# A decoder block in split precision: a padded low part of k, and the two softmax components combined on ScalarE and GpSimd

## The chip, the cores and the metric

The kernel runs on one core of one Trainium2 chip. The time is that of one execution on the device in microseconds (us): the median of several runs, and for a profile the span from the first to the last instruction.

A core has five engines that matter here. TensorE (PE) multiplies matrices; its weight loads are listed apart (PEld). VectorE (DVE), ScalarE (ACT) and GpSimd (POOL) work on tiles of up to 128 partitions. SyncE (SP) and ACT issue the DMAs. Each engine works through its instructions in order.

## The reference, cut to what matters

The input is 512 rows of 1024 numbers, in float32. After a norm, one projection gives a convolution branch, q and k (8 heads with two components of 64 each), v (8 heads of 128) and two gates. The part around the change is the differential attention:

```python
def diff_attention(q, k, v, lam):
    for i in range(seq_len // Q_BLOCK):          # 4 blocks of 128 queries
        kv_len = (i + 1) * Q_BLOCK
        s = jnp.einsum("bqhcd,bkhcd->bhcqk", qs, ks).astype(jnp.float32) * scale
        s = jnp.where(mask, s, neg)
        p = jax.nn.softmax(s, axis=-1)
        a = p[:, :, 0] - lam * p[:, :, 1]        # two components, 64 numbers each
        outs.append(jnp.einsum("bhqk,bkhe->bqhe", a.astype(v.dtype), vs))
```

Then the heads are normed and projected, gated together with the convolution branch (31 taps per channel, a layer norm, SiLU, a projection), projected, and a feed-forward layer of 2816 and a last norm follow.

## The kernel before

*Split precision.* A float32 matrix is kept as a high part (rounded to the matmul's format, fp32r) and a low part (the rest), and a product is three matmuls: high by high, low by high, high by low. Weights arrive in units of 512 KB (tile wr); ACT casts the high part (wh), and POOL (for units 3 to 63) or DVE subtracts for the low part (wl), three units ahead of their use (`next_unit`, lines 341 to 348).

*Stages.* The convolution's input projections; then eight heads, each with its q and k projection and, every second head, a v projection; the gates, with the norm of the heads; the projections; the feed-forward layer. The convolution's taps (one DVE instruction each, from `conv_ops`) fill DVE through the heads.

*The scores.* For a head, `softmaxes` (lines 610 to 675) packs high and low of q into one tile of 128 rows per component: qs2[c] has the high part of q in its own 64 rows and the low part in the other 64. kd[c] holds the high part of k twice. So one matmul of 128 rows gives high by high plus low by high. The third product, high of q by low of k, is a matmul of 64 rows (line 641), since kl holds both components, 64 rows each. A block i has (i+1) x 128 columns and four such matmuls, two for each component.

*The softmax.* For each component DVE adds the mask and takes the row maximum in one instruction (line 644, a custom one in the profile), multiplies the maximum by -0.125 (a one-column TENSOR_SCALAR), and ACT takes the exponential and its sum. `combine` then has two reciprocals, one multiplication by lambda (lamc), a multiplication of component 1 on ACT, and the combination on DVE (line 664). `outputs` transposes the result on PE, splits it (ACT and DVE) and multiplies by v.

*What sets the order.* Python generators with a model of each engine's clock (class `Model`, lines 80 to 121, costs in `Engine`, lines 142 to 162) record the program: a generator yields until the model says that its operands are ready, and `pump` puts taps on DVE whenever its modelled clock falls behind PE's. So fewer or cheaper instructions on one engine move others as well. Nothing is reordered on the chip.

Of the kernel before, what the change touches and what calls it, by code (L numbers as in the profile page):

```python
# [4 lines left out]
T = 512  # L5
D = 1024
P = 128
NH = 8
HD = 64
# [158 lines left out]
def build(nw):  # L168
# [10 lines left out]
    nc = bacc.Bacc("TRN2", target_bir_lowering=False, num_devices=1)  # L179
# [12 lines left out]
    need = model.need  # L192
    clk = model.clk

    with tile.TileContext(nc) as tc, contextlib.ExitStack() as homes:
# [3 lines left out]
        with tc.tile_pool(name="cn", bufs=1) as cn, \  # L199
# [88 lines left out]
            def until_room(tag, n, reserve=0):  # L288
                while live[tag] + n + reserve > BUFS[tag]:
                    yield now[0] + 0.3  # L290
# [164 lines left out]
            G.memset(mhalf, -0.5)  # L455
            make_identity(nc, ident)
# [153 lines left out]
            def softmaxes(h, qk):  # L610
                yield need(*qk)

                qm, km = qk
                yield from until_room("T4", 5)
                qs2 = [tl("T4", F32R) for _ in range(2)]
                kd = [tl("T4", F32R) for _ in range(2)]
                kl = tl("T4", F32R)
# [4 lines left out]
                for c in range(2):  # L622
                    S.copy(kd[c][half[1 - c]], km[half[c]])
                    V.tensor_tensor(out=qs2[c][half[1 - c]], in0=qm[half[c]], in1=f32(qs2[c])[half[c]], op=ALU.subtract)
                    V.tensor_tensor(out=kl[half[c]], in0=km[half[c]], in1=f32(kd[c])[half[c]], op=ALU.subtract)
# [5 lines left out]
                def scores(i):  # L631
                    kv = (i + 1) * P
                    pm, rs = [], []
                    for c in range(2):
                        cp = slice(c * HD, (c + 1) * HD)
                        qs = slice(i * P, (i + 1) * P)
                        yield from until_room("T5", 1, 5)
                        s_ps = psum("at")
                        yield need(s_ps, qs2[c], kd[c], kl)
                        mm(s_ps[:, :kv], qs2[c][:, qs], kd[c][:, :kv], True, False)  # L640
                        mm(s_ps[:, :kv], qs2[c][cp, qs], kl[cp, :kv], False, True)
                        sm = tl("T5")
                        mx, den = small(), small()
                        V.tensor_tensor_reduce(out=sm[:, :kv], in0=s_ps[:, :kv], in1=mask[:, T - kv:], op0=ALU.add,
                                               op1=ALU.max, scale=1.0, scalar=-3.4e38, accum_out=mx)
                        V.tensor_scalar(out=mx, in0=mx, scalar1=-0.125, scalar2=None, op0=ALU.mult)
                        S.activation(sm[:, :kv], sm[:, :kv], AF.Exp, bias=mx, scale=0.125, accum_out=den)
                        pm.append(sm)
                        rs.append(den)
                    prob[i] = (pm, rs)  # L650

                def combine(i):
                    kv = (i + 1) * P
                    pm, rs = prob.pop(i)
                    yield need(*rs)
                    for c in (1, 0):
                        r = small()
                        V.reciprocal(r, rs[c])
                        rs[c] = r
                        if c == 1:  # L660
                            V.tensor_tensor(out=r, in0=r, in1=lamc, op=ALU.mult)
                            S.mul(pm[1][:, :kv], pm[1][:, :kv], mul=r)
                    yield need(pm[1])
                    V.scalar_tensor_tensor(out=pm[0][:, :kv], in0=pm[0][:, :kv], scalar=rs[0], in1=pm[1][:, :kv],
                                           op0=ALU.mult, op1=ALU.subtract)
                    drop("T5")
                    probs[h][i] = pm[0]
# [5 lines left out]
                drop("T4", 5)  # L673
# [386 lines left out]
```

## Time and profile before

| | |
|---|---|
| median of 3 runs | 927.87 us (927.46 to 928.8) |
| the profiled execution | 927.44 us |
| its span | 925.1 us |
| busy PE, DVE, ACT, POOL | 903.1, 593.5, 375.9, 261.9 us |
| mean granted TensorE clock | 0.994 |

Busy times overlap, since the engines work beside each other; only the engine that is never idle sets the time by its own work. Nearly all instructions are recorded at line 141 or by one helper, so rows are told apart by tile names: "mm", "at" and "cv" are PSUM tiles (projections, attention, convolution), "T" is any SBUF tile, "sm" a column. A matmul is shown with its start and a modelled length that overlaps the next one; what it costs in a stream is the distance from start to start.

### The profile page before, as it was taken

What the parts mean: (1) busy time and instruction counts of PE and PEld (TensorE: products, weight loads), DVE (VectorE), ACT (ScalarE), POOL (GpSimd) and SP (SyncE); (2) the same over time, 40 slices, a digit from 0 to 9 for tenths busy, and PEclk for the clock granted to TensorE, in tenths of its full rate; (3) what the DMA queues carried; (4) which work ended last, traced back from release to release, by engine and by line L of the source; (5) the groups of instructions that cost most, each with busy time, mean ns of one, the idle gap of its engine ahead of it and who ended that gap; (6) DMA issues with size and microseconds to landing.
All of it is one profiled execution on the core that took longest, in us unless ns stands there. A gap on an engine that the chain in (4) does not pass through costs nothing.

```text
span 925.1 us, 11231 instructions
## 1 busy us (share of the span) xinstructions
PE 903.1 (98%) x4246; PEld 735.4 (79%) x4246; DVE 593.5 (64%) x1048; ACT 375.9 (41%) x615; POOL 261.9 (28%) x211
## 2 busy tenths in 40 slices
PE   8989999999999999999999999999999999999996
PEld 5868888777787777768788888888888888888885
DVE  6599999898899889996766563333443434422422
ACT  7232336565555786444532442323322232311312
POOL 1654465563645526536200001011111111100000
PEclk9899999999999999999999999999999999999999
DMA  7223222121122222222223342222223332322302
GB/s 273 88 81 106 90 92 69 46 91 46 46 70 69 69 69 69 72 89 81 102 79 126 137 137 92 91 91 91 91 91 111 102 107 92 114 91 91 113 24 91
DMA packets 26150, 85.19 MB, mean 92 GB/s; under 512 B 3041, under 2 KB 3809, under 8 KB 26097
## 3 DMA queue, kind: packets, MB, share of 16 engines
q1 hardware_dynamic: 24944, 82.52, 26.6%
q10 hardware_dynamic: 1152, 1.97, 0.6%
q8 instruction: 33, 0.54, 0.2%
q14 instruction: 21, 0.16, 0.1%
HBM read 82.38 MB, written 2.10 MB: 91 GB/s over the span
## 4 chain that ended last, share of the span: by engine, by line
PE 84%; DVE 9%; ACT 2%; issue 2%; POOL 1%; DMA 1%; SPq 0%; POOLq 0%; ACTq 0%; DVEq 0%
PE mm L141 51%; PE at L141 29%; DVE T L141 7%; PE cv L141 4%; ACT T L141 2%; DVE cv L141 1%; POOL wl L141 1%; DVE sm L141 1%; DMA wr<-wall 1%; ACT wh L141 0%; DMA T<-xT 0%; DVE dg L141 0%; SPq L233 0%; POOL T L141 0%; POOL rc L141 0%
## 5 line engine op out<-in xcount | busy, mean ns | idle before, releaser
L141 PE MATMUL mm<-T,wh 128*128 128x512 f32 x1360 | 427.6, 395 | 3.7 <-DVE T L141 3.2
L141 PEld LDWEIGHTS mm<-T,wh 128*128 128x128 f32 x1360 | 250.0, 188 | 60.3 <-issue 4.6
L141 PE MATMUL mm<-T,wl 128*128 128x512 f32 x680 | 265.7, 391 | 0.5 <-DVE wl L141 0.5
L141 POOL TENSOR_TENSOR wl<-wr,wh 128x512 fp32r<-128x512 f32 x122 | 165.2, 1381 | 172.0 <-ACT wh L141 171.1
L141 ACT CAST wh<-wr 128x1024 fp32r<-128x1024 f32 (+1 forms) x148 | 148.7, 1031 | 71.3 <-PE cv L141 35.3
L141 DVE SCALAR_TENSOR_TENSOR cv<-T,vec_sb,cv 128x512 f32<-128x512 f32 x232 | 160.3, 746 | 0.1
L141 POOL TENSOR_TENSOR T<-T,T 128x512 f32<-128x512 f32 x64 | 84.7, 1325 | 253.7 <-DVE T L141 230.9
L141 PE MATMUL at<-T,wh 128*128 128x512 f32 x496 | 154.4, 393 | 0.0
L141 PEld LDWEIGHTS mm<-T,wl 128*128 128x128 f32 x680 | 127.8, 188 | 28.7 <-DVE wl L141 1.0
L141 DVE TENSOR_TENSOR wl<-wr,wh 128x1024 fp32r<-128x1024 f32 (+1 forms) x88 | 102.0, 1186 | 70.1 <-ACT wh L141 69.7
L141 DVE TENSOR_TENSOR T<-T,T 128x512 fp32r<-128x512 f32 (+2 forms) x127 | 101.6, 801 | 58.9 <-ACT T L141 56.8
L141 ACT CAST T<-T 128x512 fp32r<-128x512 f32 (+2 forms) x112 | 67.5, 617 | 132.9 <-POOL T L141 82.1
L141 PEld LDWEIGHTS at<-T,wh 128*128 128x128 f32 x496 | 93.7, 190 | 19.5
L141 DVE TENSOR_TENSOR T<-mm,T 128x512 f32<-128x512 f32 (+1 forms) x76 | 51.7, 682 | 83.3 <-PE mm L141 73.7
L141 PE MATMUL mm<-wh,T 128*128 128x256 f32 (+1 forms) x432 | 101.2, 318 | 0.0
L141 PE MATMUL at<-T,wl 128*128 128x512 f32 x248 | 97.1, 392 | 0.0
L141 ACT ACTIVATE T<-T 128x512 f32<-128x512 f32 (+1 forms) x66 | 40.4, 622 | 131.9 <-DVE T L141 131.9
L141 ACT ACTIVATE T<-T,sm 128x128 f32<-128x128 f32 (+3 forms) x100 | 56.7, 567 | 81.3 <-DVE sm L141 77.5
L141 PEld LDWEIGHTS mm<-wh,T 128*128 128x128 f32 x432 | 73.0, 190 | 7.0 <-issue 1.3
L141 DVE TENSOR_TENSOR T<-at,T 128x512 f32<-128x512 f32 (+4 forms) x59 | 38.0, 649 | 62.4 <-PE at L141 56.1
L141 PE MATMUL at<-T,T 128*128 128x256 f32 (+8 forms) x288 | 68.2, 334 | 1.2 <-DVE T L141 1.2
L141 PE MATMUL mm<-wl,T 128*128 128x256 f32 (+1 forms) x216 | 68.1, 315 | 0.0
(85 smaller groups left out, 641.3 us busy)
## 6 DMA issues: line engine op xcount, KB each, us to landing
wr<-wall SPq DMA_DIRECT2D x145, 512.0 KB, 3.2
T<-xT SPq DMA_DIRECT2D x16, 256.0 KB, 4.6
out<-T ACTq DMA_DIRECT2D x4, 256.0 KB, 2.8
out<-T SPq DMA_DIRECT2D x4, 256.0 KB, 2.6
wr<-wall SPq DMA_DIRECT2D x4, 128.0 KB, 4.4
T<-cs ACTq DMA_DIRECT2D x2, 256.0 KB, 4.7
T<-gfin SPq DMA_DIRECT2D x2, 256.0 KB, 3.6
T<-mask ACTq DMA_DIRECT2D x1, 256.0 KB, 5.1
```

The lines of the kernel that those rows point to most:

```text
L141: r = f(*args, **kw)
```

## The change

The low part of k gets a tile of 128 rows for each component (kz, two sets, used by heads in turn), whose other 64 rows are set to zero once at the start. The matmul of line 641 so has 128 rows in place of 64: the other half of qs2[c] meets zeros. The row maximum is taken as a minimum of the scores times -0.125, so that the separate multiplication goes; both sums of a block share one tile of two columns, with one reciprocal; the multiplication by lambda is a TENSOR_SCALAR; ACT multiplies both components, and POOL subtracts them. The planner asks for four tiles of "T4" in place of five, and waits for the head before the last. The scratch for dynamic DMAs is set to 1024.

```diff
--- before.py
+++ after.py
@@ -176,7 +176,7 @@
     AF, ALU = mybir.ActivationFunctionType, mybir.AluOpType
     AX = mybir.AxisListType
 
-    nc = bacc.Bacc("TRN2", target_bir_lowering=False, num_devices=1)
+    nc = bacc.Bacc("TRN2", target_bir_lowering=False, num_devices=1, dynamic_dma_scratch_size=1024)
     xT_d = nc.dram_tensor("xT", [8, P, T], F32, kind="ExternalInput").ap()
     w_d = nc.dram_tensor("wall", [nw, P, 1024], F32, kind="ExternalInput").ap()
     vec_d = nc.dram_tensor("vec", [P, NVEC], F32, kind="ExternalInput").ap()
@@ -453,6 +453,10 @@
                 G.memset(f32(pick)[:, 9 * h:9 * h + 1], 1.0)
             G.memset(ones, 1.0)
             G.memset(mhalf, -0.5)
+            kz = [[cn.tile([P, T], F32R, name=f"kz{b}{c}") for c in range(2)] for b in range(2)]
+            for b in range(2):
+                for c in range(2):
+                    G.memset(f32(kz[b][c])[(1 - c) * HD:(2 - c) * HD], 0.0)
             make_identity(nc, ident)
             load(vec, vec_d)
             ss = SumSq("T3", V)
@@ -610,11 +614,14 @@
             def softmaxes(h, qk):
                 yield need(*qk)
 
+
                 qm, km = qk
-                yield from until_room("T4", 5)
+                yield from until_room("T4", 4)
+                while started[0] < h - 2:
+                    yield now[0] + 0.5
                 qs2 = [tl("T4", F32R) for _ in range(2)]
                 kd = [tl("T4", F32R) for _ in range(2)]
-                kl = tl("T4", F32R)
+                kl = kz[h % 2]
                 half = [slice(0, HD), slice(HD, P)]
                 for c in range(2):
                     S.copy(qs2[c][half[c]], qm[half[c]])
@@ -622,7 +629,7 @@
                 for c in range(2):
                     S.copy(kd[c][half[1 - c]], km[half[c]])
                     V.tensor_tensor(out=qs2[c][half[1 - c]], in0=qm[half[c]], in1=f32(qs2[c])[half[c]], op=ALU.subtract)
-                    V.tensor_tensor(out=kl[half[c]], in0=km[half[c]], in1=f32(kd[c])[half[c]], op=ALU.subtract)
+                    V.tensor_tensor(out=kl[c][half[c]], in0=km[half[c]], in1=f32(kd[c])[half[c]], op=ALU.subtract)
                 drop("T5", 2)
                 while started[0] < h - 1:
                     yield now[0] + 0.5
@@ -630,39 +637,34 @@
 
                 def scores(i):
                     kv = (i + 1) * P
-                    pm, rs = [], []
+                    pm, den = [], small(2)
                     for c in range(2):
-                        cp = slice(c * HD, (c + 1) * HD)
                         qs = slice(i * P, (i + 1) * P)
                         yield from until_room("T5", 1, 5)
                         s_ps = psum("at")
-                        yield need(s_ps, qs2[c], kd[c], kl)
+                        yield need(s_ps, qs2[c], kd[c], kl[c])
                         mm(s_ps[:, :kv], qs2[c][:, qs], kd[c][:, :kv], True, False)
-                        mm(s_ps[:, :kv], qs2[c][cp, qs], kl[cp, :kv], False, True)
+                        mm(s_ps[:, :kv], qs2[c][:, qs], kl[c][:, :kv], False, True)
                         sm = tl("T5")
-                        mx, den = small(), small()
+
+                        mx = small()
                         V.tensor_tensor_reduce(out=sm[:, :kv], in0=s_ps[:, :kv], in1=mask[:, T - kv:], op0=ALU.add,
-                                               op1=ALU.max, scale=1.0, scalar=-3.4e38, accum_out=mx)
-                        V.tensor_scalar(out=mx, in0=mx, scalar1=-0.125, scalar2=None, op0=ALU.mult)
-                        S.activation(sm[:, :kv], sm[:, :kv], AF.Exp, bias=mx, scale=0.125, accum_out=den)
+                                               op1=ALU.min, scale=-0.125, scalar=3.4e38, accum_out=mx)
+                        S.activation(sm[:, :kv], sm[:, :kv], AF.Exp, bias=mx, scale=-1.0, accum_out=den[:, c:c + 1])
                         pm.append(sm)
-                        rs.append(den)
-                    prob[i] = (pm, rs)
+                    prob[i] = (pm, den)
 
                 def combine(i):
                     kv = (i + 1) * P
-                    pm, rs = prob.pop(i)
-                    yield need(*rs)
+                    pm, den = prob.pop(i)
+                    yield need(den)
+                    r = small(2)
+                    V.reciprocal(r, den)
+                    V.tensor_scalar(out=r[:, 1:2], in0=r[:, 1:2], scalar1=lamc, scalar2=None, op0=ALU.mult)
                     for c in (1, 0):
-                        r = small()
-                        V.reciprocal(r, rs[c])
-                        rs[c] = r
-                        if c == 1:
-                            V.tensor_tensor(out=r, in0=r, in1=lamc, op=ALU.mult)
-                            S.mul(pm[1][:, :kv], pm[1][:, :kv], mul=r)
-                    yield need(pm[1])
-                    V.scalar_tensor_tensor(out=pm[0][:, :kv], in0=pm[0][:, :kv], scalar=rs[0], in1=pm[1][:, :kv],
-                                           op0=ALU.mult, op1=ALU.subtract)
+                        S.mul(pm[c][:, :kv], pm[c][:, :kv], mul=r[:, c:c + 1])
+                    yield need(*pm)
+                    G.tensor_tensor(out=pm[0][:, :kv], in0=pm[0][:, :kv], in1=pm[1][:, :kv], op=ALU.subtract)
                     drop("T5")
                     probs[h][i] = pm[0]
 
@@ -670,7 +672,7 @@
                     yield from scores(i)
                     if i:
                         yield from combine(i - 1)
-                drop("T4", 5)
+                drop("T4", 4)
                 yield from combine(3)
                 started[0] = h
```

On PE the order of the last block of head 0, before (at_ tiles are the scores; T_194 and T_195 are kd, T_196 is kl; mm_1320 is the v projection that runs around it):

```order
L141 MATMUL mm_1320<-wh_1172,T_88_455 128x256
L141 MATMUL at_1397<-T_194_1201,T_192_1199 128x512
L141 MATMUL at_1397<-T_196_1203,T_192_1199 128x512
L141 MATMUL at_1406<-T_195_1202,T_193_1200 128x512
L141 MATMUL at_1406<-T_196_1203,T_193_1200 128x512
L141 MATMUL mm_1320<-wh_1172,T_89_464 128x256
```

And in the changed kernel, where kz_154 and kz_155 stand for kl:

```order
L141 MATMUL mm_1321<-wh_1180,T_83_442 128x256
L141 MATMUL at_1376<-T_194_1209,T_192_1207 128x512
L141 MATMUL at_1376<-kz_154,T_192_1207 128x512
L141 MATMUL at_1383<-T_195_1210,T_193_1208 128x512
L141 MATMUL at_1383<-kz_155,T_193_1208 128x512
L141 MATMUL mm_1321<-wh_1180,T_87_461 128x256
```

The four matmuls stay in place; the second and fourth read another tile.

On DVE the stretch between the score reductions (ISA) of the third and the fourth block of head 0, before (cv_ are convolution taps; T_211 is the combination of the second block):

```order
L141 TENSOR_SCALAR sm_1343<-sm_1343 128x1
L141 RECIPROCAL sm_1348<-sm_1284 128x1
L141 TENSOR_TENSOR sm_1348<-sm_1348,lamc 128x1
L141 RECIPROCAL sm_1352<-sm_1269 128x1
L141 SCALAR_TENSOR_TENSOR cv_888<-T_113_595,vec_sb,cv_888 128x512
L141 TENSOR_TENSOR T_241_1376<-T_202_1243,T_241_1376 64x512
L141 SCALAR_TENSOR_TENSOR cv_840<-T_96_494,vec_sb,cv_840 128x512
L141 SCALAR_TENSOR_TENSOR cv_888<-T_113_595,vec_sb,cv_888 128x512
L141 TENSOR_TENSOR T_245_1380<-T_221_1302,T_243_1378 64x512
L141 TENSOR_TENSOR T_242_1377<-T_202_1243,T_242_1377 64x512
L141 TENSOR_TENSOR T_245_1380<-T_221_1302,T_244_1379 64x512
L141 SCALAR_TENSOR_TENSOR T_211_1267<-T_211_1267,sm_1352,T_215_1282 128x256
```

The same place now, up to the fourth block's reductions:

```order
L141 ISA sm_1340 128x1
L141 RECIPROCAL sm_1343<-sm_1268 128x2
L141 TENSOR_SCALAR sm_1343<-sm_1343,lamc 128x1
L141 SCALAR_TENSOR_TENSOR cv_848<-T_96_502,vec_sb,cv_848 128x512
L141 SCALAR_TENSOR_TENSOR cv_896<-T_113_603,vec_sb,cv_896 128x512
L141 ISA T_237_1379,sm_1380<-at_1376,T_3_100 128x512
L141 ISA sm_1380 128x1
L141 ISA T_240_1386,sm_1387<-at_1383,T_3_100 128x512
L141 ISA sm_1387 128x1
L141 RECIPROCAL sm_1390<-sm_1328 128x2
L141 TENSOR_SCALAR sm_1390<-sm_1390,lamc 128x1
```

The combination and the multiplications of the maxima are gone, one reciprocal of two columns stands for two, and the splits of the next head's q and k come after the reductions.

On POOL the stretch of head 3 in the changed kernel (wl_ are halves of weights; the pairs with T_2_99 and after it are rope; the others, T_469, T_478, T_486 and T_505, are the new subtractions of the four blocks):

```order
L141 TENSOR_TENSOR wl_2387<-wr_2183,wh_2385 128x512 x2
L141 TENSOR_TENSOR T_472_2426<-T_472_2426,T_2_99 128x512
L141 TENSOR_TENSOR T_473_2428<-T_473_2428,T_472_2426 128x512
L141 TENSOR_TENSOR T_469_2415<-T_469_2415,T_474_2440 128x128
L141 TENSOR_TENSOR T_492_2506<-T_492_2506,T_2_99 128x512
L141 TENSOR_TENSOR T_493_2508<-T_493_2508,T_492_2506 128x512
L141 TENSOR_TENSOR wl_2516<-wr_2313,wh_2514 128x512 x2
L141 TENSOR_TENSOR wl_2523<-wr_2383,wh_2521 128x512 x2
L141 TENSOR_TENSOR T_478_2448<-T_478_2448,T_481_2455 128x256
L141 TENSOR_TENSOR T_486_2487<-T_486_2487,T_489_2494 128x384
L141 TENSOR_TENSOR T_505_2546<-T_505_2546,T_508_2553 128x512
```

Before, the same part of the queue had weights and rope alone:

```order
L141 TENSOR_TENSOR wl_2362<-wr_2133,wh_2360 128x512 x2
L141 TENSOR_TENSOR wl_2410<-wr_2236,wh_2408 128x512 x2
L141 TENSOR_TENSOR T_505_2461<-T_505_2461,T_2_99 128x512
L141 TENSOR_TENSOR T_506_2463<-T_506_2463,T_505_2461 128x512
L141 TENSOR_TENSOR T_511_2488<-T_511_2488,T_2_99 128x512
L141 TENSOR_TENSOR T_512_2490<-T_512_2490,T_511_2488 128x512
L141 TENSOR_TENSOR wl_2498<-wr_2358,wh_2496 128x512 x2
```

The subtractions stand between weights and rope, and each waits for two multiplications on ACT.

## Rows read from the trace of the kernel before

**Rows 1.** The page, busy time by engine: busy us (share of the span), instructions.

```profile
PE 903.1 (98%) x4246; PEld 735.4 (79%) x4246; DVE 593.5 (64%) x1048; ACT 375.9 (41%) x615; POOL 261.9 (28%) x211
```

**Rows 2.** Windows, 125 to 350 us: length, then busy us (instructions) PE, PEld, DVE, ACT, POOL.

```profile
125.00:350.00 225.00, 220.09 (x1135) 175.06 (x1135) 201.56 (x514) 138.51 (x290) 116.39 (x88) 1.00 0.19 64
```

**Rows 3.** Chain that ended last: start us, length us, what, how many; a regular run.

```profile
475.46 10.88 PE at L141 x48
```

**Rows 4.** Timeline of PE, 256 columns: start us, length us, engine, instruction, form, count.

```profile
261.74 0.28 PE L141 MATMUL mm<-wh,T 128*128 128x256 f32 x1
...
262.33 0.28 PE L141 MATMUL mm<-wh,T 128*128 128x256 f32 x1
```

**Rows 5.** Timeline of PE around the last block of the last head.

```profile
341.30 1.66 PE L141 MATMUL at<-T,T 128*128 128x512 f32 x4
342.89 0.55 PE L141 MATMUL at<-ident,T 128*128 128x128 f32 x3
343.19 0.71 PE L141 MATMUL mm<-T,wh 128*128 128x512 f32 x2
```

**Rows 6.** Waits of weight loads, 125 to 350 us: us in total, times, longest.

```profile
PEld at L141 <- issue: 13.1, 58, 0.4
PEld at L141 <- DVE T L141: 7.6, 10, 1.8
```

**Rows 7.** Waits of PE, 125 to 350 us.

```profile
PE at L141 <- DVE T L141: 4.9, 6, 1.5
```

**Rows 8.** Timeline of PE: transposes of probabilities, in brackets the idle time before.

```profile
184.97 0.87 PE L141 MATMUL at<-ident,T 128*128 128x128 f32 x6 [1.47 <-DVE T L141]
```

**Rows 9.** Timeline of PE around a third block (384 columns).

```profile
314.08 1.44 PE L141 MATMUL at<-T,T 128*128 128x384 f32 x4
315.44 0.73 PE L141 MATMUL mm<-T,wh 128*128 128x512 f32 x2
```

**Rows 10.** Timeline of PE: pairs of a first block (128 columns) and a second (256).

```profile
216.56 0.48 PE L141 MATMUL at<-T,T 128*128 128x128 f32 x2
216.97 0.73 PE L141 MATMUL mm<-T,wh 128*128 128x512 f32 x2
...
219.22 0.68 PE L141 MATMUL at<-T,T 128*128 128x256 f32 x2
219.82 0.44 PE L141 MATMUL at<-ident,T 128*128 128x128 f32 x2
```

**Rows 11.** Groups of DVE, 125 to 350 us: xcount | busy us, mean ns | idle before.

```profile
L141 DVE SCALAR_TENSOR_TENSOR cv<-T,vec_sb,cv 128x512 f32<-128x512 f32 x82 | 58.1, 743 | 0.0
...
L141 DVE TENSOR_TENSOR sm<-sm,lamc 128x1 f32<-128x1 f32 x32 | 15.7, 492 | 1.1
...
L141 DVE TENSOR_SCALAR sm<-sm 128x1 f32<-128x1 f32 x64 | 9.8, 154 | 2.2
L141 DVE RECIPROCAL sm<-sm 128x1 f32<-128x1 f32 x64 | 9.8, 153 | 0.0
...
L141 DVE SCALAR_TENSOR_TENSOR T<-T,sm,T 128x384 f32<-128x384 f32 x8 | 6.8, 855 | 0.0
L141 DVE SCALAR_TENSOR_TENSOR T<-T,sm,T 128x512 f32<-128x512 f32 x8 | 6.8, 853 | 0.5 <-ACT T L141 0.2
...
L141 DVE SCALAR_TENSOR_TENSOR T<-T,sm,T 128x256 f32<-128x256 f32 x8 | 5.3, 660 | 0.5 <-ACT T L141 0.3
...
L141 DVE SCALAR_TENSOR_TENSOR T<-T,sm,T 128x128 f32<-128x128 f32 x8 | 4.8, 604 | 1.4 <-ACT T L141 1.4
```

**Rows 12.** Groups of ACT, 125 to 350 us: exponentials and multiplications of 512 columns.

```profile
L141 ACT ACTIVATE T<-T,sm 128x512 f32<-128x512 f32 x24 | 17.3, 723 | 35.6 <-DVE sm L141 35.6
```

**Rows 13.** Groups of POOL, 125 to 350 us.

```profile
L141 POOL TENSOR_TENSOR wl<-wr,wh 128x512 fp32r<-128x512 f32 x54 | 73.0, 1376 | 83.4 <-ACT wh L141 83.4
L141 POOL TENSOR_TENSOR T<-T,T 128x512 f32<-128x512 f32 x34 | 45.5, 1341 | 25.2 <-DVE T L141 23.8
```

**Rows 14.** Timeline of POOL at the start: its first wl.

```profile
20.36 5.89 POOL L141 TENSOR_TENSOR wl<-wr,wh 128x512 fp32r<-128x512 f32 x4 [18.38 <-ACT wh L141]
```

## The prediction

> **What bounds the kernel now.** I read the busy times of the page first: TensorE (PE) is busy 98% of the span [rows 1], so time can only leave through PE: through instructions that take less of it, or through gaps. Next the stretch that the change touches, the eight heads, from 125 to 350 us [rows 2]: PE is busy 220.1 of 225 us and VectorE (DVE) 201.6, ScalarE (ACT) 138.5, GpSimd (POOL) 116.4. PE is the bound there, DVE a close second, and the other two have room. The granted clock is 1.00 through the stretch, so no part of the time is the clock's.
>
> Busy does not mean well used. In the timeline of PE I compare starts, since the shown lengths overlap. A run of 48 matmuls of 512 columns takes 10.88 us [rows 3], 0.227 us each. Five matmuls of 256 columns in the middle of a projection take from 261.74 to 262.33, 0.118 us each [rows 4]. Three transposes of 128 columns run from 342.89 to 343.19, 0.10 us each [rows 5]. These are the regular prices; 384 columns, which have no regular run, I put midway between 256 and 512, at 0.173 us (an estimate). The score matmuls do not keep to them. The four of the last block (two with 128 rows, two with 64, in turn) run from 341.30 to 342.89 [rows 5]: 1.59 us where four regular ones take 0.91. So each pair of a 128-row and a 64-row matmul loses 0.34 us. The same is seen in the waits: weight loads for "at" sat 13.1 us on "issue", in 58 pieces, though nothing in the profile holds them [rows 6].
>
> Last, the gaps. PE waits for a DVE result 4.9 us in six places of the stretch, its weight loads 7.6 us in ten [rows 6, 7]. The longest is the transpose of probabilities at 184.97, held 1.47 us [rows 8].
>
> **The change, part by part.** *Padded low part of k.* The second matmul of a pair reads 128 rows, half of them zeros, so no matmul of the scores has 64 rows. Count, columns and order of the four matmuls stay. What goes is the loss, block by block, per head:
> - 512 columns: 1.59 - 4 x 0.227 = 0.68 us [rows 3, 5].
> - 384: 315.44 - 314.08 = 1.36, less 4 x 0.173 = 0.69: 0.67 us [rows 9].
> - 256: one pair takes 219.82 - 219.22 = 0.60, less 2 x 0.118 = 0.24: 0.36, and two pairs 0.72 us [rows 4, 10].
> - 128: one pair takes 216.97 - 216.56 = 0.41, less 2 x 0.10: 0.21, and two pairs 0.42 us [rows 5, 10].
>
> Sum 2.49 us per head, 19.9 us for eight. The bound below is the 13.1 us of idle weight loads, which leave out what the matmuls themselves lose while they drain; above, all 32 blocks at 0.68 us, 21.8 us. I take 19.9. All of it is on the path, since PE is it.
>
> The Trainium skill has a rule against this and one for it. "TensorE: Matmul & The Clock Gate", in the section on why this matters for kernels, says that one small-K matmul takes the time of one with K=128, that is, columns alone count; read alone, padding would give nothing, and this term would be 0. "TensorEngine Tiling (Array Packing)", Tiling Modes, says that a change of tiling mode drains the engine; by that the loss is in the change from 128 to 64 rows and back, and all of it goes. The trace agrees with the second: the loss per pair is nearly the same from 256 to 512 columns (0.36, 0.34 and 0.34 us), as a price per change would be and one per column would not.
>
> *Fewer small DVE instructions.* From the stretch [rows 11]: 64 TENSOR_SCALAR at 154 ns go, 9.8 us; of 64 RECIPROCAL 32 go, 4.9 us; 32 TENSOR_TENSOR with lamc, 15.7 us, become 32 TENSOR_SCALAR of one column, at 154 ns 4.9 us, which saves 10.8; 32 SCALAR_TENSOR_TENSOR leave DVE, 6.8 + 6.8 + 5.3 + 4.8 = 23.7 us. Sum 49.2 us. The planner sees a lighter DVE and puts more of the convolution's taps among the heads: counted in the two orders, 198 stand before the last score reduction instead of 169. 29 taps at 743 ns [rows 11] are 21.5 us. DVE so falls by 27.7 us, to 174 of some 204 us. None of this is on the path but through the gaps, since taps have no early reader.
>
> *ACT and POOL.* ACT gets 32 multiplications. At the 0.723 us of the 512-column group [rows 12] they are at most 23.1 us; by size (a quarter each of 128 to 512 columns) about 14.5 us. ACT goes to some 153 to 162 of 204 us. POOL gets 32 subtractions: at 1.341 us each [rows 13] at most 42.9 us, by size 26.8. POOL goes to 143 to 159 us of 204. Both have cover. What stands behind a waiting subtraction on POOL are the halves of the weights' low part (wl) and the two instructions of rope; POOL sat 83.4 us of the stretch waiting for ACT's cast before a wl [rows 13], so these can be later by a few us without PE seeing it. If that cover were gone, each late pair would hold PE by up to 2 x 1.376 = 2.75 us.
>
> What replaces the DVE combination is longer: for 512 columns one more multiplication (0.72) and a subtraction of 1.34 for one of 0.85 [rows 11 to 13], 1.2 us more, and at worst a wl pair in front, 2.75 us: 4.0 us. Against this the planner moved the transposes back. Counted in the two orders as matmuls of 512 columns, PE has between the last scores of a head and the transposes of its last two blocks 30 to 58 others before, and 48 to 79 now. The least room is 18 matmuls larger, 18 x 0.227 = 4.1 us, just the worst case. So the gaps behind the combinations should shrink. On the other side three splits of transposed probabilities have less room (6 to 8 matmuls, 1.4 to 1.8 us), and may hold PE about 1 us each. I set the gaps, 6 us now (between 4.9 and 7.6), at 4.5: 1.5 us off. The ends: all go, -6; or 16 combinations (two a head) hold PE 0.75 us each, +12 - 6 = +6 us.
>
> A rule of "Perfetto Trace Analysis", Optimizing Scalar/DVE Operations, speaks against the move: GpSimd and DVE share a read port of SBUF, so work moved between them may not help. The trace agrees that they hold each other up: the one-column TENSOR_TENSOR with lamc takes 492 ns on average, a one-column TENSOR_SCALAR 154 [rows 11]. But the change also takes 64 such two-operand instructions off DVE, so by the rule too DVE does not lose.
>
> *The rest at nothing.* The four memsets of 64x512 on POOL come at the start, where POOL sits 18.38 us before its first wl at 20.36 [rows 14]; even at 1.341 us each they are 5.4 us and hidden, and without that cover would delay that wl by as much. Writing the padded tile waits for the reads of two heads before, about two heads, 2 x 28 us, back (225 us hold eight heads). The smaller DMA scratch has no row; I take 0. The order of the weights' loads does not change.
>
> **Sum.** Span 925.1 - 19.9 - 1.5 = 903.7 us. The profiled execution took 927.44, 2.3 more than its span, and the median is 927.87. 903.7 + 2.3 = 906.0 us. Measured against the median it would be 0.4 more, which I leave in the range.
>
> **The rivals.**
> *Half the gain is given back in the new chain (A).* For it: DVE was already 90% busy, and the combination now crosses three engines and POOL's queue. Against it: the larger room counted above. Each of 16 combinations holds PE 0.6 us beyond today's gaps: 9.6 us, so 906.0 + 1.5 + 9.6 = 917, say 911 to 921.
> *The pause stays (B).* It belongs to something else than the row count, such as two matmuls that share their moving operand's tile or bank; or columns alone set the price. For it: no 128-row pair with these operands is in the trace. Against it: the regular streams also gather in one bank and pay nothing. The time would be 927.4 - 1.5 = 926, or 922 to 929.
> *The POOL chain sets the pace (C), slower.* If each of the two combinations a head waits for one whole wl pair that stands ahead of it, 16 x 2.75 = 44 us come for 19.9 + 6 that go: 927.4 + 18 = 945 us. It decides from 26 / 16 = 1.6 us per combination. For it: POOL works in order, and in head 3 four wl halves and a rope stand between two subtractions. Against it: the room of 48 matmuls (10.9 us) and POOL at most 78% busy.
> *More is gained (D).* With a lighter DVE all gaps of the stretch go: 925.1 - 19.9 - 6 + 2.3 = 901.5, with the upper bound of the first term 899.6.
>
> **How the numbers follow.** Forecast with 902 to 911 around it: 0.68. D: 0.10. A: 0.12. B: 0.05, of which 0.02 within 0.2% (1.9 us, about what a measurement of this kernel can tell from no change). C: 0.05. Faster by over 0.2% is 0.68 + 0.10 + 0.12 + 0.03 = 0.93, within 0.02, slower 0.05. The range from 899 to 916 takes in the forecast, D and half of A, 0.84.
>
> **What would show it.** In the profile after: no 64-row form in PE's groups, four 512-column score matmuls from start to start in 0.91 us, and "issue" gone from the waits of "at" but for the 8-row matmuls of the head norm. DVE's groups without the 32 combinations and with some 32 one-column TENSOR_SCALAR at about 154 ns. PE's waits name POOL T instead of DVE T, in total under 6 us. The forecast is wrong if PE waits for POOL or ACT by more than 10 us in the stretch, if the padded pairs still take 0.8 us at 512 columns, or if the gap before the gates grows by what the heads gained.

## The result: 0.5% faster, 923.2 us where 906 were predicted

| kernel | median us | ratio to before [95% interval] |
|---|---|---|
| before | 927.46 (925.39 to 928.8) | 1 |
| changed | 923.19 (920.19 to 924.81) | 0.9948 [0.9935, 0.9961] |
| changed, run again | 920.78 (919.35 to 923.82) | 0.9939 [0.9923, 0.9955] |

One execution of the changed kernel, the profiled one, took 1778.84 us with matmuls of 512 columns 0.445 us from start to start in place of 0.227; it counts in the median of seven, 923.19 (921.8 without it), and is left out of the range and the ratio. All rows of "after" below come from a second profile of the same kernel (span 917.9 us, execution 920.04 us). So 4.3 us are gained in the first measurement and 6.3 in the second (where before had 927.04), of the 21.4 that were forecast. By time alone 923.2 lies in the range of rival B (the pause stays) and 920.8 in that of A (half given back); the profile has to decide.

I read the page and the stretch of the heads first, against [rows 1, 2]: busy us by engine, then length, busy us (instructions) of PE, PEld, DVE, ACT, POOL, and the granted clock.

```profile
PE 887.2 (97%) x4246; PEld 734.6 (80%) x4246; DVE 558.9 (61%) x920; ACT 387.8 (42%) x647; POOL 293.6 (32%) x247
...
125.00:350.00 225.00, 211.68 (x1169) 180.65 (x1168) 202.22 (x438) 154.88 (x330) 153.21 (x124) 0.98 0.20 66
```

PE now idles 13.3 us of the 225 (4.9 before). DVE is as busy as before, with 76 instructions fewer: the planner filled what was freed. (The stretch reaches 15 us further into the program than before, since the last score reduction now stands at 328.3 us and not at 343.6; up to there DVE is busy 181.8 of 203.3 us now, and 195.4 of 218.6 before, 89% both.) And the clock is no longer 1.00.

What the change was to remove is gone. The timeline of PE around a fourth block (start, length) answers to [rows 5]:

```profile
164.47 0.39 PE L141 MATMUL at<-T,T 128*128 128x512 f32 x1
164.70 0.40 PE L141 MATMUL at<-kz,T 128*128 128x512 f32 x1
164.93 0.40 PE L141 MATMUL at<-T,T 128*128 128x512 f32 x1
165.17 0.39 PE L141 MATMUL at<-kz,T 128*128 128x512 f32 x1
165.39 0.63 PE L141 MATMUL mm<-T,wh 128*128 128x512 f32 x2
```

Four score matmuls run from 164.47 to 165.39, 0.92 us where it was 1.59. Now the waits of PE and of its weight loads from 125 to 350 us, which answer to [rows 6, 7]: us in total, times, longest.

```profile
PE at L141 <- DVE T L141: 6.2, 6, 2.4
PE at L141 <- DVE sm L141: 2.6, 4, 1.0
PE at L141 <- DVE kz L141: 2.4, 3, 1.3
PE at L141 <- POOL T L141: 1.8, 2, 1.0
...
PEld at L141 <- issue: 0.5, 2, 0.3
```

"issue" fell from 13.1 to 0.5. But PE waits for DVE 11.2 us, in three forms: T (splits, and rope, the rotation of q and k by position), sm (the reductions free a score bank) and kz (the split of k). Before, it was T alone, 4.9.

To put a size on this I went through the matmuls of one profiled execution of each kernel from 60 to 460 us and summed, start to start, what each took over its regular price: the row changes (a matmul next to one with another number of rows; those that stay, 2.6 us, are the 8-row matmuls of the head norm), the gaps of over 0.3 us, and the extra time in stretches at half clock.

| 60 to 460 us | row changes | gaps | low clock | rest |
|---|---|---|---|---|
| before | 23.1 | 8.4 | 0 | 8.3 |
| after | 2.6 | 18.4 | 4.0 | 9.2 |
| before with the padding alone | 2.6 | 29.1 | 4.4 | 7.5 |
| after without the padding | 21.3 | 12.6 | 6.0 | 9.3 |
| after, combination on DVE | 2.6 | 15.4 | 1.5 | 9.1 |
| after, taps dearer for the planner | 2.6 | 13.5 | 0 | 8.1 |

20.5 us leave with the row changes, 10.0 come back as gaps, 4.0 as a lower clock, 0.9 in the rest: 5.6 net. Between the two profiled executions lie 7.4 us, between the medians 6.3.

One place shows how. In the timeline of head 1 of after (brackets: idle time before, and for what):

```profile
179.65 1.57 DVE L141 TENSOR_TENSOR kz<-T,T 64x512 fp32r<-64x512 f32 x1
...
181.25 1.68 DVE L141 TENSOR_TENSOR T<-T,T 64x512 fp32r<-64x512 f32 x1
181.27 0.33 PE L141 MATMUL at<-kz,T 128*128 128x128 f32 x1 [0.84 <-DVE kz L141]
...
182.34 3.41 POOL L141 TENSOR_TENSOR wl<-wr,wh 128x512 fp32r<-128x512 f32 x2
182.95 1.66 DVE L141 TENSOR_TENSOR kz<-T,T 64x512 fp32r<-64x512 f32 x1
184.65 1.16 DVE L141 TENSOR_TENSOR T<-at,T 128x512 fp32r<-128x512 f32 x2
185.39 1.03 PE L141 MATMUL at<-T,T 128*128 128x256 f32 x7 [1.69 <-DVE T L141]
...
187.50 0.58 PE L141 MATMUL at<-T,T 128*128 128x256 f32 x1 [0.59 <-DVE sm L141]
```

DVE takes the low parts of q and k of the head (the splits), each 1.57 to 1.68 us; only then comes the split of transposed probabilities at 184.65, for which PE has waited 1.69 us at 185.39. The windows around it:

```profile
175.00:186.00 11.00, 8.47 (x45) 6.61 (x45) 10.84 (x15) 5.69 (x10) 10.67 (x8) 1.00 0.16 50
...
187.00:193.00 6.00, 5.50 (x17) 4.73 (x18) 2.89 (x11) 3.50 (x10) 2.30 (x2) 0.50 0.22 82
193.00:200.00 7.00, 7.00 (x52) 6.73 (x52) 5.94 (x14) 5.72 (x12) 5.64 (x5) 0.97 0.00 0
```

DVE and POOL are busy 10.84 and 10.67 of 11 us while PE has 8.47. Behind these waits the granted clock falls to 0.50 (1.2 GHz) for some 7 us, with PE busy again 5.50 of 6; then it is back. Before had no such stretch among the heads.

The groups of DVE and POOL, 125 to 350 us, answer to [rows 11, 13]: xcount | busy us, mean ns | idle before.

```profile
L141 DVE SCALAR_TENSOR_TENSOR cv<-T,vec_sb,cv 128x512 f32<-128x512 f32 x127 | 88.3, 747 | 0.0
L141 DVE TENSOR_TENSOR T<-T,T 64x512 fp32r<-64x512 f32 x16 | 19.1, 1195 | 3.4 <-ACT T L141 3.0
L141 DVE TENSOR_TENSOR kz<-T,T 64x512 fp32r<-64x512 f32 x16 | 18.4, 1151 | 0.4
...
L141 DVE TENSOR_SCALAR sm<-sm,lamc 128x1 f32<-128x1 f32 x32 | 6.9, 214 | 1.1
```

```profile
L141 POOL TENSOR_TENSOR wl<-wr,wh 128x512 fp32r<-128x512 f32 x56 | 77.0, 1398 | 45.1 <-ACT wh L141 40.4 <-issue 4.7
L141 POOL TENSOR_TENSOR T<-T,T 128x512 f32<-128x512 f32 x44 | 58.4, 1331 | 21.1 <-DVE T L141 16.4 <-ACT T L141 3.2
```

POOL has 44 instructions of that form for 34, and the smaller subtractions besides. DVE has 127 taps for 82 (29 of the 45 more stand before the last score reduction); and the 32 splits of q and k take 1173 ns on average, where the trace of before has them in one group of 901:

```profile
L141 DVE TENSOR_TENSOR T<-T,T 64x512 fp32r<-64x512 f32 x32 | 28.8, 901 | 2.7 <-ACT T L141 2.1
```

### The profile page after: what moved, and what is told of

Same layout as the page of the kernel before. It is cut to its first block, busy times and chain, and to the rows that moved or that the text cites. A ratio compares the mean times of both kernels' runs of the same rounds, so it can differ in the third digit from the quotient of the medians.

```text
span 1776.7 us, 11186 instructions
## 1 busy us (share of the span) xinstructions
PE 1768.4 (100%) x4246; PEld 1194.7 (67%) x4246; DVE 558.3 (31%) x920; ACT 392.9 (22%) x647; POOL 286.2 (16%) x247
## 4 chain that ended last, share of the span: by engine, by line
PE 99%; issue 0%; DVE 0%; ACT 0%; POOLq 0%; POOL 0%
PE mm L141 65%; PE at L141 30%; PE cv L141 5%; DVE T L141 0%; ACT T L141 0%; POOLq L195 0%; POOL sm L141 0%; DVE fs L141 0%
## 5 line engine op out<-in xcount | busy, mean ns | idle before, releaser
L141 PE MATMUL mm<-T,wh 128*128 128x512 f32 x1360 | 780.9, 678 | 0.0
L141 PEld LDWEIGHTS mm<-T,wh 128*128 128x128 f32 x1360 | 400.3, 299 | 213.7 <-issue 194.9
L141 PE MATMUL mm<-T,wl 128*128 128x512 f32 x680 | 460.6, 677 | 0.0
L141 PE MATMUL at<-T,wh 128*128 128x512 f32 x496 | 284.1, 676 | 0.0
L141 PEld LDWEIGHTS mm<-T,wl 128*128 128x128 f32 x680 | 203.6, 299 | 111.9 <-issue 102.0
L141 POOL TENSOR_TENSOR T<-T,T 128x512 f32<-128x512 f32 (+3 forms) x96 | 111.8, 1169 | 632.1 <-DVE T L141 568.7
L141 PE MATMUL mm<-wh,T 128*128 128x256 f32 (+1 forms) x432 | 181.6, 512 | 0.0
L141 PE MATMUL at<-T,wl 128*128 128x512 f32 x248 | 167.2, 674 | 0.0
L141 PE MATMUL mm<-wl,T 128*128 128x256 f32 (+1 forms) x216 | 109.1, 505 | 0.0
L141 PEld LDWEIGHTS at<-T,wl 128*128 128x128 f32 x248 | 73.6, 297 | 41.7 <-issue 38.6
L141 ACT ACTIVATE T<-T,sm 128x256 f32<-128x256 f32 (+3 forms) x132 | 70.9, 560 | 128.3 <-DVE sm L141 124.5
```

The lines of the kernel that those rows point to most:

```text
L141: r = f(*args, **kw)
```

## The experiments

All are edits of before or of the changed kernel; ratios are to before, with 95% intervals.

**Each half alone.** First the changed kernel again; then before with the padding alone (the lines on kz and "T4" of the diff); the change without it (64-row kl as in line 641); and the change with the combination back on DVE:

```diff
-                        mm(s_ps[:, :kv], qs2[c][cp, qs], kl[cp, :kv], False, True)
+                        mm(s_ps[:, :kv], qs2[c][:, qs], kl[c][:, :kv], False, True)
...
-                    for c in (1, 0):
-                        S.mul(pm[c][:, :kv], pm[c][:, :kv], mul=r[:, c:c + 1])
...
-                    G.tensor_tensor(out=pm[0][:, :kv], in0=pm[0][:, :kv], in1=pm[1][:, :kv], op=ALU.subtract)
+                    S.mul(pm[1][:, :kv], pm[1][:, :kv], mul=r[:, 1:2])
...
+                    V.scalar_tensor_tensor(out=pm[0][:, :kv], in0=pm[0][:, :kv], scalar=r[:, 0:1], in1=pm[1][:, :kv],
```

> The changed kernel as it is, for a profile at the ordinary clock: the one at hand has every 512-column matmul at 0.445 us, twice the usual distance. Theory 1 (the padding does save its 20 us, and they are given back by gaps of PE and by TensorE's clock): time 920 to 924 us, four 512-column score matmuls from start to start in 0.91 us, and gaps or a stretch at the lower clock of together over 10 us that the kernel before did not have. Theory 2 (the pause between score matmuls stays): the same time, but the four matmuls still take 1.4 to 1.6 us and the gaps are those of before.

> The kernel before with the padded low part of k alone; softmax and combination as before. Theory 1: 905 to 910 us, since the 20 us of the row change go and the gaps of before stay. Theory 2: 921 to 928 us.

> The changed kernel with 64-row low-part matmuls as before; the smaller softmax and the combination on ACT and POOL stay. Theory 1: 935 to 942 us, the changed kernel plus the 20 us of the row change. Theory 2: 920 to 926 us, the same as the changed kernel.

> The changed kernel with the combination back on DVE as one SCALAR_TENSOR_TENSOR (ACT scales component 1 alone, POOL subtracts nothing). Theory 1, if POOL's queue makes the new gaps: 903 to 909 us. If the gaps are not POOL's (the clock at the start, or another wait): 918 to 923 us.

Measured: 920.78 us (0.9939 [0.9923, 0.9955]); padding alone 928.47 (1.002 [1.001, 1.0029]); no padding 933.47 (1.0072 [1.005, 1.0094]); combination on DVE 914.98 (0.9877 [0.986, 0.9893]).

Neither half gains by itself, and but for the first run no time fell where a theory had put it. The padding costs 1.4 us with the old softmax (927.04 to 928.47) and gains 12.7 with the new (933.5 to 920.8). With the padding alone the 20.5 us of row changes go and the gaps of PE take them all; its waits and its window:

```profile
PE at L141 <- DVE T L141: 19.3, 13, 2.9
PE at L141 <- DVE sm L141: 2.5, 3, 0.9
PE at L141 <- DVE kz L141: 2.4, 4, 0.7
```

```profile
125.00:350.00 225.00, 200.57 (x1114) 172.27 (x1113) 201.41 (x507) 136.07 (x287) 116.03 (x87) 0.98 0.19 62
```

PE is busy 19.5 us less than before and no earlier done; DVE's 201.4 us are those of before. I read this so: the pause of the row changes was time in which DVE's results came. With the combination back on DVE the changed kernel is 5.8 us faster; POOL is busy 126.80 us of the stretch, and the splits are quicker:

```profile
L141 DVE TENSOR_TENSOR T<-T,T 64x512 fp32r<-64x512 f32 x16 | 16.1, 1005 | 1.2 <-ACT T L141 0.7
L141 DVE TENSOR_TENSOR kz<-T,T 64x512 fp32r<-64x512 f32 x16 | 13.2, 828 | 0.5
```

But this edit moves the planner too: 173 taps stand before the last score reduction in place of 198. By the table below, 17 taps fewer gave as much with the combination still on POOL (915.0 us), and 32 fewer gave more (911.7). So it is not shown that the combination on POOL is a loss by itself.

**How many taps among the heads.** The planner's price of a tap, which decides how many it puts there, is the only edit (in the changed kernel; once with the combination on DVE):

```diff
-                    cost = 0.065 + n * (0.00116 if method == "scalar_tensor_tensor" else 0.00104)
+                    cost = 0.065 + n * (0.0015 if method == "scalar_tensor_tensor" else 0.00104)
```

> The changed kernel with one number of the planner's model changed: a convolution tap of 512 columns is priced at 0.83 us in place of 0.66 (it takes 0.75 on the chip). The planner then puts 166 taps among the heads in place of 198; the instructions are the same. Theory 3 (DVE is late because the planner fills the time that the change freed with taps, so PE now waits for DVE where it paused before): DVE's lateness falls, 905 to 914 us. Theory 4 (PE's new waits come of POOL's queue and of the lock between POOL and DVE, whatever the taps): 918 to 922 us.

> The changed kernel with the combination on DVE and a tap priced at 0.83 us: 141 taps among the heads in place of 173. Theory 3: 901 to 909 us, below the 915 us with the old price. Theory 4: 913 to 917 us, since POOL's part is out already and taps do not matter.

> The changed kernel with a tap priced at 0.75 us, what it takes: 181 taps among the heads, between the 198 of the changed kernel (920 us) and the 166 of the price of 0.83 (912 us). Theory 3: between the two, 912 to 920 us. Theory 4: no order by taps.

> The changed kernel with a tap priced at 0.99 us: 142 taps among the heads. Theory 3: fewer gaps in the heads than with 166, but the taps that are left delay the layer norm of the convolution, and PE waits 10 to 30 us at it near 450 us: 915 to 935 us. Theory 4: 918 to 922 us.

| price per column | taps before the last score reduction | median us | ratio |
|---|---|---|---|
| 0.00116 (changed kernel) | 198 | 920.78 | 0.9939 [0.9923, 0.9955] |
| 0.00133 | 181 | 915.01 | 0.9867 [0.9831, 0.9904] |
| 0.0015 | 166 | 911.65 | 0.9815 [0.9788, 0.9841] |
| 0.0018 | 142 | 935.04 | 1.008 [1.0054, 1.0106] |
| 0.0015, combination on DVE | 141 | 931.7 | 1.0048 [1.0035, 1.0062] |

With 32 taps fewer the changed kernel gains 9.1 us more and is the best version of all, ahead of both kernels. Part of that is the clock: the profiled execution, 906.8 us, has no stretch at low clock in the heads, and three of the other four took 911.7 to 912.9 us at a mean granted clock of 0.991 to 0.993 in place of its 0.998. Its waits and its window:

```profile
PE at L141 <- DVE T L141: 4.3, 5, 2.0
PE at L141 <- DVE kz L141: 2.2, 2, 1.3
```

```profile
125.00:350.00 225.00, 214.60 (x1205) 182.53 (x1205) 193.10 (x422) 164.34 (x346) 155.75 (x127) 1.00 0.21 69
```

With still fewer the taps come too late for the convolution's layer norm. PE with 0.0018, 430 to 480 us:

```profile
PE cv L141 <- DVE T L141: 14.0, 1, 14.0
PE at L141 <- DVE T L141: 9.6, 1, 9.6
PE mm L141 <- ACT T L141: 2.8, 1, 2.8
```

The version with the combination on DVE failed there too (4.1 + 9.6 + 1.7 + 2.8 us), which I had not foreseen.

**Measured prices for all DVE instructions.** The planner's prices raised, with the padding and without:

```diff
+                elif n <= 4:
+                    cost = 0.2
...
+                    cost = 0.15 + n * 0.00116 + 0.15 * (method == "tensor_tensor_reduce")
```

> The kernel before with the padded low part of k alone, and the planner's DVE prices raised to what the trace shows (a one-column instruction 0.2 us, others 0.15 us plus 1.16 ns a column, the score reduction 0.15 us more). Theory 3: the padding's 20 us show once DVE is on time, 903 to 912 us. Theory 4: 922 to 930 us, as with the old prices.

> The kernel before with the same raised prices and no padding, the partner of the run with padding and raised prices. Theory 3: 921 to 926 us, since the few gaps of before shrink and the pause between score matmuls stays, so that the padding is worth 14 to 20 us between the two. Theory 4: 925 to 929 us, with no difference between the two.

Measured: 964.56 us with the padding (1.0403 [1.0389, 1.0417]), 974.2 without (1.0506 [1.0491, 1.052]). Both were spoiled by the gaps at the layer norm just seen (waits of 24.1 and 28.1 us); that the padding is worth 9.6 us between them says little.

**Half of the taps left out.** Every second tap is not computed, in before and with the padding:

```diff
-                return [first] + [tap(k) for k in range(1, CW)]
+                return [first] + [tap(k) for k in range(2, CW, 2)]
```

> The kernel before with every second convolution tap left out (16 of 31 instructions per channel tile stay), so that DVE has some 90 us less to do before the layer norm of the convolution. Theory 3 (DVE is a second bound of the heads, late by what the planner loads on it): the gaps of 8 us shrink, the row change stays: 917 to 924 us. Theory 4 (POOL's queue and its lock with DVE make the waits): 924 to 928 us.

> The same with the padded low part of k (every second tap left out here too). Theory 3: with DVE on time the padding is worth 16 to 21 us, so 898 to 906 us, where with all taps it was worth nothing (928.5 against 927). Theory 4: within 8 us of the run without padding.

Measured: 930.96 us (1.004 [1.0027, 1.0054]) and 926.49 (0.9985 [0.9971, 0.9998]). The padding is worth 4.5 us: better than -1.4, far from 20. What that says of DVE's load must be read by stretches. The planner puts the taps that are left in front, so until 250 us DVE is nearly as busy as with all of them (111.1 of 125 us; 112.8 with the padding alone), and its load isn't tested there. Later it has a third of its time free:

```profile
125.00:250.00 125.00, 112.19 (x631) 97.67 (x630) 111.07 (x277) 71.07 (x158) 71.65 (x53) 0.96 0.19 64
250.00:350.00 100.00, 92.32 (x509) 78.08 (x509) 65.01 (x186) 68.56 (x136) 45.99 (x35) 1.00 0.19 64
```

From 250 to 350 us PE still idles 7.7 of 100 us, and 0.7 without the padding. So at least there it isn't DVE's load alone, as the third theory has it. Why before itself is 3.9 us slower with half of its taps left out is not shown in full; PE is busy 22.16 of the 25 us from 125 on, at a granted clock of 0.86, where it was 25.00 at 1.00.

The padded version's timeline in this stretch shows what a light DVE is late with:

```profile
285.02 0.56 DVE L141 TENSOR_TENSOR T<-at,T 128x384 fp32r<-128x384 f32 x1 [1.42 <-ACT T L141]
...
286.33 2.86 POOL L141 TENSOR_TENSOR T<-T,T 128x512 f32<-128x512 f32 x2 [3.52 <-DVE T L141]
...
288.15 1.05 DVE L141 TENSOR_TENSOR sm<-sm,lamc 128x1 f32<-128x1 f32 x1
...
290.06 0.91 DVE L141 SCALAR_TENSOR_TENSOR T<-T,sm,T 128x512 f32<-128x512 f32 x1 [0.78 <-ACT T L141]
...
291.02 0.87 PE L141 MATMUL at<-ident,T 128*128 128x128 f32 x6 [1.85 <-DVE T L141]
```

DVE waits for ACT in its order (1.42, 0.78 us) and its one-column multiplication by lambda, elsewhere 0.16 us, lasts 1.05 us and ends as POOL's pair does, at 289.2. Then the transposes are 1.85 us late.

**The one-column multiplication.** The padding alone, with this instruction as the change has it; the order on all engines stays:

```diff
-                            V.tensor_tensor(out=r, in0=r, in1=lamc, op=ALU.mult)
+                            V.tensor_scalar(out=r, in0=r, scalar1=lamc, scalar2=None, op0=ALU.mult)
```

> The kernel before with the padding alone and the 32 one-column TENSOR_TENSOR with lamc as one-column TENSOR_SCALAR, all else in the same order on every engine. Theory 4: the instruction falls from about 0.5 to 0.2 us and the gaps behind it shrink by 6 to 10 us, 917 to 923 us. Theory 5: within 3 us of 928.5 us.

Measured: 928.59 us (1.0016 [1.0005, 1.0028]); padding alone had 928.47. The group with the edit, and the one without it:

```profile
L141 DVE TENSOR_SCALAR sm<-sm,lamc 128x1 f32<-128x1 f32 x32 | 6.9, 214 | 1.1
```

```profile
L141 DVE TENSOR_TENSOR sm<-sm,lamc 128x1 f32<-128x1 f32 x32 | 18.9, 590 | 1.1
```

It saves DVE 12.0 us there and the gaps 3.0 (29.1 to 26.1), and the time nothing; the 32 splits of q and k, at 1088 ns in place of 924, take 5.2 of the 12.0 back. The fourth theory (POOL alone, whatever the taps) had 6 to 10 us for this edit and none for the price of the taps, which gave 9.1.

**Transposes and products later in PE's order.** Here the planner lets 3 and 1.5 us pass (or half) before it issues what reads a combination:

```diff
-                    yield need(tp, *[av[i] for _, i in grp])
+                    yield need(tp, *[av[i] for _, i in grp]) + 3.0
...
-                    yield need(o_ps, ah, al, *[t for v in vhl for t in v])
+                    yield need(o_ps, ah, al, *[t for v in vhl for t in v]) + 1.5
```

> The kernel before with the padded low part of k alone, and the planner told to put the transposes 3 us and the products with v 1.5 us later than its model says (161 taps among the heads, as without). Theory 5 (placement: PE comes to the transposes before the softmax chain is through, and the pause that the padding removes had been hidden waiting): the gaps of 29 us shrink to 10 or less, 906 to 914 us. Theory 4 (lock and queues make the chain longer whatever the place): over 922 us.

> The changed kernel with the transposes 1.5 us and the products with v 0.75 us later in the plan (197 taps among the heads, as before). Theory 5: fewer gaps and no stretch at the lower clock in the heads, 905 to 914 us. Theory 4: 918 to 923 us.

> The changed kernel with a tap priced at 0.83 us and the same delays. Theory 5: both help, 900 to 908 us. If the taps' price did by itself what the delay does: 908 to 913 us, as with the price alone.

> The padding alone, every second convolution tap left out, and the transposes 3 us and products with v 1.5 us later in the plan. Theory 6 (two things hold PE in the heads, each enough by itself: DVE's queue while it is full of taps, and the place of the transposes where it is not): with both eased the gaps fall below 14 us, 905 to 917 us, and the padding is worth 14 to 21 us against the partner. Theory 4 (lock and in-order waits on DVE as such): 922 to 930 us, as with either alone.

> The partner without the padding: every second tap left out, the same delays. Theory 6: 924 to 932 us, since the pause between score matmuls stays and the gaps of before were small. Theory 4: the same.

| kernel | median us | ratio |
|---|---|---|
| padding alone, 3 and 1.5 | 930.04 | 1.0048 [1.0027, 1.0069] |
| changed, 1.5 and 0.75 | 916.54 | 0.9892 [0.9867, 0.9918] |
| changed with tap price 0.0015, 1.5 and 0.75 | 915.56 | 0.9876 [0.9861, 0.9892] |
| padding and half of the taps, 3 and 1.5 | 925.26 | 0.9985 [0.9973, 0.9998] |
| before with half of the taps, 3 and 1.5 | 933.28 | 1.0061 [1.0043, 1.008] |

The waits of the padding alone with the delay, 125 to 350 us:

```profile
PE at L141 <- DVE sm L141: 6.8, 5, 2.1
PE at L141 <- DVE T L141: 5.3, 4, 2.4
PE at L141 <- DVE cv L141: 2.2, 2, 1.6
PE at L141 <- DVE kz L141: 2.1, 4, 1.0
PE at L141 <- ACT wh L141: 1.6, 1, 1.6
PE at L141 <- ACT T L141: 1.6, 2, 1.2
```

"DVE T" fell from 19.3 to 5.3, and four others rose; the sum of the gaps from 60 to 460 us is 28.7 for 29.1. The waits moved, against the fifth theory. The changed kernel gained 4.2 us, its gaps 19.8 for 18.4, but with no stretch at low clock among the heads: it gained by the clock, not by fewer gaps. With the dearer taps the delay loses 3.9 us (911.65 to 915.56), outside both expectations. Halved taps and the delay together, the sixth theory, make the padding worth 8.0 us, not 20; until 250 us DVE is busy 109.1 of 125 us there too.

## Why the prediction was wrong

*What bounds the kernel.* That PE is the bound in busy time was right; that only PE's own work could set the time was not. DVE, at 201.6 of 225 us [rows 2], was almost as long, and its results have readers on PE in every block. The experiment with the padding alone shows that PE's work was not what set the time: it fell by 19.5 us in the stretch and the time rose by 1.4. That DVE's load is what set it instead is argued, and with the halved taps it is not the whole.

*The row changes* (-19.9 us): right, 20.5 measured, and none left but the 8-row ones. The rule of the Trainium skill that I followed ("TensorEngine Tiling (Array Packing)", Tiling Modes) is borne out by 0.92 us for four 512-column matmuls.

*The gaps* (6 us set at 4.5, "1.5 us off"): this is the step that failed. From 60 to 460 us they went from 8.4 to 18.4, and behind them came 4.0 us at low clock, for which the sum had no term: +14 in place of -1.5, 15.5 us of error for 14.8 between 906.0 and 920.8. But for three splits of probabilities, put at about 1 us each, it asked only whether the chain of the combination had room in PE's order, counted in matmuls; but with PE 20 us faster every DVE result has less time. Its sign, POOL T in place of DVE T in PE's waits, failed (DVE 11.2 us, POOL 1.8), and none of its three signs of being wrong came. The chain's end at POOL was indeed no trouble: PE waited for POOL 1.8 us, its weight loads 3.5. The upper end of the term, +6, was too near as well.

*Fewer DVE instructions* (-49.2 + 21.5 = -27.7 us): the counts came out, the 29 taps among them, but "174 of some 204 us" did not. The 204 us from 125 on, in the same columns as above:

```profile
125.00:329.00 204.00, 190.88 (x1065) 163.51 (x1064) 182.48 (x407) 138.61 (x305) 141.25 (x114) 0.97 0.20 65
```

DVE is busy 182.5 us, 8.5 more than said, and the splits of q and k alone take 32 x (1173 - 901) ns = 8.7 us more than before. That "taps have no early reader" is true, and was the wrong question: what stands behind a tap in DVE's queue has one. The row of the tap prices speaks for it, 198 to 166 taps for 9.1 us, part of it the clock. The multiplication by lambda takes 214 ns, not 154, a small miss of 1.9 us.

*ACT and POOL:* 138.6 (153 to 162 said) and 141.3 us (143 to 159 said) in the same 204 us: less than said, so the cover was there. Not priced was what POOL's work does to DVE. The Trainium skill's rule on the shared port ("Perfetto Trace Analysis", Optimizing Scalar/DVE Operations) was weighed and put aside because 64 two-operand instructions left DVE; the splits had still to share with POOL. The trace agrees for them: the 16 splits of before and the 6 of after that no POOL instruction overlaps take 682 to 690 ns, those beside POOL up to 1686. How much of the time this costs isn't separated, since the run with the combination on DVE was 5.8 us faster with 25 taps fewer as well.

*The rest at nothing:* right. The four memsets take 2.21 us together at 1.52 us, and the first wl starts at 20.71 (20.36 before), behind ACT's cast.

*The rivals.* B falls by the 0.92 us, though its range holds the first time of 923.2: by luck, since its mechanism did not come. C falls by POOL's 1.8 us, D by the gaps. A (917, at most 921) came near the second time and named half of the reason: not 16 combinations late by 0.6 us, but waits for reductions, splits and rope.

*What stays open* is which part of DVE's lateness is the order of its queue (with the halved taps and the delay the next head's splits of q and k stand before the fourth block's reductions, at 254.7 and 259.5 us), which its waits for ACT, and which POOL. The multiplication by lambda and the place of the transposes, as far as the delays moved them, are each excluded as the whole; the load by itself only from 250 us on. One reading that no run tests: the planner's price of a matmul has no row change in it, so before, PE ran behind the plan in the heads and DVE's results had that time; without the row changes PE keeps to the plan, and DVE, whose taps are priced too low, does not.

## What to carry to other kernels

When two engines feed each other at 98% and 90% busy, shortening the work of the first may be worth only what the second can follow: look at what reads the second's results in each block, and price the edit as if the second became the bound. Take filler work off the second engine's queue in the same step (here 9 us came back that way, part of them the clock's), but not so much that it is late for its own reader. Work moved to an engine with room can slow the engine it was to relieve; compare the mean duration of the same instruction in both traces.

## What the runs showed of the hardware

- A drop of the granted clock to 0.50 followed groups of waits of PE of 0.6 to 1.7 us (187 to 193 us in after), with PE nearly busy again; it costs about 4 us in the heads of after and nothing there in the profiled execution of the best version.
- A split of 64x512 took 682 ns at the least in before, 901 on average with POOL busy 52% of the stretch and 1173 with POOL busy 68%. The share is not all: at 52% the run with the cheaper multiplication by lambda had 1088. What no POOL instruction overlapped took 682 to 690 ns in both kernels, and the taps 728 to 754 whatever POOL did. A one-column multiplication took 590 ns as TENSOR_TENSOR and 214 as TENSOR_SCALAR in otherwise equal kernels.
- One execution of 1778.84 us ran its matmuls of 512 columns at half speed while its rows give the granted clock as 1.00. With PE so slow its waits for DVE were nearly gone: 1.4 us in the whole run, where the second profile has 20.7.
